# RMSNorm with each row written twice: engines issue in written order, and the last tile is loaded and stored in halves

## The chip, the cores and the metric

One core of one Trainium2 chip. The metric is the device time of one execution in microseconds (us). The kernel before takes 240.31 us, the median of 3 runs (239.82 to 240.62).

## The reference

```python
def reference(x, gamma):                     # x: 8 x 512 x 2048 f32
    x_rep = np.repeat(x, 2, axis=1)
    rms = np.sqrt((x_rep ** 2).mean(axis=-1, keepdims=True) + 1e-6)
    x_norm = x_rep / rms
    return (x_norm * gamma[None, None, :]).astype(np.float32)   # 8 x 1024 x 2048 f32
```

Every row is normalized and appears twice in the output. So 33.6 MB must be read and 67.1 MB written, whatever the kernel does in between.

## The kernel before

The 4096 rows are cut into 8 tiles of 128 partitions x 4 rows. A buffer `y` has 8 row slots for each partition: a tile is loaded into slots 4 to 7, and its 8 output rows are built in place in slots 0 to 7, so that one store moves 64 KB of consecutive bytes for each partition. There are three such buffers. (In the code `K = 4` is the rows of a partition in a tile and `R = 2` the copies of each row.) ACT (the scalar engine) squares and sums a row and takes the root, DVE (the vector engine) takes the reciprocal and scales; ACT copies three of the four rows, DVE the last.

```python
    load(0, parts=K)                       # K = 4, R = 2; load() issues on nc.sync
    # ... gamma to all partitions, eps ...
    load(1)
    load(2)
    for i in range(ntiles):                # 8 tiles
        y = ys[i]
        for k in range(K):
            xk = y[:, K * (R - 1) + k, :]
            y0, y1 = y[:, R * k, :], y[:, R * k + 1, :]
            # ... sq, ss, rms, rstd ...
            nc.scalar.activation(out=sq[:], in_=xk, func=Act.Square, accum_out=ss[:])
            nc.scalar.activation(out=rms[:], in_=ss[:], func=Act.Sqrt, scale=inv_d, bias=eps_t[:])
            nc.vector.reciprocal(out=rstd[:], in_=rms[:])
            nc.vector.scalar_tensor_tensor(out=y0, in0=xk, scalar=rstd[:], in1=gamma_b[:],
                                           op0=Alu.mult, op1=Alu.mult)
            if k == K - 1:
                nc.vector.tensor_copy(out=y1, in_=y0)
            else:
                nc.scalar.copy(out=y1, in_=y0)
        nc.sync.dma_start(out=out_t[i], in_=y.rearrange("p j d -> p (j d)"))
        if i >= 1 and i + 2 < ntiles:
            load(i + 2)
```

SyncE (SP) issues the large transfers, which run one after another in one queue, q1, on 16 DMA engines. A packet is the piece of a transfer that one DMA engine moves at a time; a transfer has landed when all its packets are done. Slack is how much earlier a transfer is issued than the engines run out of earlier work.

A scheduler decides in which order each engine issues these instructions. On ACT it had chosen, for most tiles: square, root, square, root, square, copy, copy, root, square, root, copy.

Of the kernel before, what the change touches and what calls it, by code (L numbers as in the profile page):

```python
# [1 line left out]

# [4 lines left out]


@with_exitstack
def kernel(  # L10
    ctx: ExitStack,
    tc: tile.TileContext,
    x: bass.AP,
    gamma: bass.AP,
    out: bass.AP,
):
    nc = tc.nc
    P = nc.NUM_PARTITIONS
    f32 = mybir.dt.float32
    Act = mybir.ActivationFunctionType  # L20
    Alu = mybir.AluOpType

    B, S, D = x.shape
    Bo, So, Do = out.shape
    R = So // S
    assert R == 2 and D == Do and B == Bo and So == S * R
    eps = 1e-6
    inv_d = 1.0 / float(D)


    K = 4
    N = B * S
    assert N % (P * K) == 0
    ntiles = N // (P * K)
    x_t = x.rearrange("b s d -> (b s) d").rearrange("(n p k) d -> n p k d", p=P, k=K)
    out_t = out.rearrange("b s d -> (b s) d").rearrange("(n p j) d -> n p (j d)", p=P, j=K * R)

    singles = ctx.enter_context(tc.tile_pool(name="singles", bufs=1))
    rows = ctx.enter_context(tc.tile_pool(name="rows", bufs=3))
    junk = ctx.enter_context(tc.tile_pool(name="junk", bufs=1, space=bass.MemoryType.PSUM))  # L40
    small = ctx.enter_context(tc.tile_pool(name="small", bufs=8))

    ys = []

    def load(i, parts=1):


        y = rows.tile([P, K * R, D], f32, name="y")
        step = K // parts
        for k in range(0, K, step):  # L50
            at = K * (R - 1) + k
            nc.sync.dma_start(out=y[:, at : at + step, :], in_=x_t[i, :, k : k + step, :])  # L52
        ys.append(y)

    load(0, parts=K)
    gamma_b = singles.tile([P, D], f32, name="gamma_b")
    nc.scalar.dma_start(out=gamma_b[0:1, :], in_=gamma.partition_broadcast(1))
    nc.gpsimd.partition_broadcast(out_ap=gamma_b[:], in_ap=gamma_b[0:1, :])  # L58
    eps_t = singles.tile([P, 1], f32, name="eps_t")
    nc.vector.memset(eps_t, eps)  # L60
    load(1)
    load(2)

    for i in range(ntiles):
        y = ys[i]
        for k in range(K):
            xk = y[:, K * (R - 1) + k, :]
            y0, y1 = y[:, R * k, :], y[:, R * k + 1, :]
            sq = junk.tile([P, D], f32, name="sq")
            ss = small.tile([P, 1], f32, name="ss")  # L70
            nc.scalar.activation(out=sq[:], in_=xk, func=Act.Square, accum_out=ss[:])  # L71
            rms = small.tile([P, 1], f32, name="rms")
            nc.scalar.activation(out=rms[:], in_=ss[:], func=Act.Sqrt, scale=inv_d, bias=eps_t[:])  # L73
            rstd = small.tile([P, 1], f32, name="rstd")
            nc.vector.reciprocal(out=rstd[:], in_=rms[:])  # L75
            nc.vector.scalar_tensor_tensor(  # L76
                out=y0, in0=xk, scalar=rstd[:], in1=gamma_b[:],
                op0=Alu.mult, op1=Alu.mult,
            )
            if k == K - 1:  # L80
                nc.vector.tensor_copy(out=y1, in_=y0)  # L81
            else:
                nc.scalar.copy(out=y1, in_=y0)  # L83
        nc.sync.dma_start(out=out_t[i], in_=y.rearrange("p j d -> p (j d)"))  # L84
        if i >= 1 and i + 2 < ntiles:
            load(i + 2)


# [1 line left out]
_INS = ['x', 'gamma']  # L90
_OUTS = [((8, 1024, 2048), 'float32')]


# [23 lines left out]
```

## Time and profile before

| What | Value | Where it is read |
|---|---|---|
| span of the profiled run | 239.1 us | page |
| busy: DMA queue q1, ACT, DVE | 98.3%, 49%, 37% | page |
| bytes moved, mean rate | 100.69 MB, 421 GB/s | page |
| one 64 KB packet on one DMA engine | 2.418 us (median of 1024) | packet records of the trace |
| last landing of load 7; last store issued | 199.38; 215.97 us | timeline |

From the page of the kernel before: the span; busy time, share and number of instructions of ACT; the DMA busy tenths in 40 slices; the DMA queues; and the chain that ended last.

```profile
span 239.1 us, 293 instructions
...
DVE 88.8 (37%) x73; ACT 116.3 (49%) x122; POOL 2.5 (1%) x5
...
DMA  7999998989899999899898999899989899898984
...
q1 hardware_dynamic: 2736, 100.66, 98.3%
...
HBM read 33.56 MB, written 67.11 MB: 421 GB/s over the span
## 4 chain that ended last, share of the span: by engine, by line
DMA 68%; ACT 13%; DVE 8%; SPq 1%; issue 1%
```

The chain gives ACT and DVE 21% of the span. It would be wrong to read this as 50 us to be won: the chain follows one path back, and while ACT and DVE work on it the DMA slices still show 8 or 9 tenths, since transfers issued earlier are draining. q1's 98.3% says how little time has no transfer.

The SyncE's timeline of the kernel before (start, duration, instruction) shows how far ahead transfers are issued:

```profile
98.53 0.33 SPq L84 DMA_DIRECT2D out_dram<-y  x1
101.38 0.34 SPq L52 DMA_DIRECT2D y<-in_x_dram  x1
127.68 0.33 SPq L84 DMA_DIRECT2D out_dram<-y  x1
...
215.97 0.33 SPq L84 DMA_DIRECT2D out_dram<-y  x1
```

Store 3 is issued at 98.53, while store 2 and load 4 lie ahead of it in the same queue and keep the engines until 110 us. The last line is different: store 7 is issued at 215.97 and the engines finish store 6 between 216.4 and 218.3 us. It is the only store with hardly any slack. The page's slices are too coarse to show it, and a table by windows books a whole packet at one moment. So the busy engines were counted from the starts and durations in the packet records; this is such a count, in half microseconds from 215.0 us:

```
before   215.0-: 16.0  16.0  15.8  11.0  15.8  16.0  16.0  16.0   engines of 16
```

### The profile page before, as it was taken

To read this page: it belongs to the slowest core of one execution; us is meant where nothing else is said; L and a number is where in the kernel's file an instruction comes from. 1 tells how busy PE (TensorE), PEld (TensorE's weight loads), DVE (VectorE), ACT (ScalarE), POOL (GpSimd) and SP (SyncE) were. 2 spreads that over 40 slices of the span, in tenths; PEclk is the share of its full clock that TensorE was granted. 3 is DMA by queue.
4 is the path that set the end of the run, shared out by engine and by line. 5 is a ranking of instruction groups with operands and counts; after the bars stand their busy time and mean duration, and the time that the engine had idled before them with its cause. 6 is when DMAs were issued, how large, how long until landed. Compare 5 with 4: busy or idle time off the path is not lost.

```text
span 239.1 us, 293 instructions
## 1 busy us (share of the span) xinstructions
DVE 88.8 (37%) x73; ACT 116.3 (49%) x122; POOL 2.5 (1%) x5
## 2 busy tenths in 40 slices
DVE  0449759590000085400863016820168202591000
ACT  2998999950000299104990059800598006970000
POOL 4000000000000000000000000000000000000000
DMA  7999998989899999899898999899989899898984
GB/s 262 426 454 439 439 439 351 526 351 526 351 428 439 493 395 451 384 411 510 362 515 351 439 439 506 373 422 433 493 384 471 362 461 461 384 482 384 493 384 175
DMA packets 2741, 100.69 MB, mean 421 GB/s; under 512 B 306, under 2 KB 306, under 8 KB 306
## 3 DMA queue, kind: packets, MB, share of 16 engines
q1 hardware_dynamic: 2736, 100.66, 98.3%
q14 instruction: 3, 0.02, 0.0%
q10 hardware_dynamic: 2, 0.01, 0.0%
HBM read 33.56 MB, written 67.11 MB: 421 GB/s over the span
## 4 chain that ended last, share of the span: by engine, by line
DMA 68%; ACT 13%; DVE 8%; SPq 1%; issue 1%
DMA y<-in_x_dram 41%; DMA out_dram<-y 27%; ACT sq L71 7%; DVE y L76 6%; ACT y L83 5%; DVE y L81 2%; SPq L52 1%; ACT rms L73 1%; DVE rstd L75 0%; SPq L84 0%
## 5 line engine op out<-in xcount | busy, mean ns | idle before, releaser
L71 ACT ACTIVATE sq<-y 128x2048 f32<-128x2048 f32 x32 | 59.7, 1865 | 92.5 <-DMA y<-in_x_dram 92.5
L76 DVE SCALAR_TENSOR_TENSOR y<-y,rstd,gamma_b 128x2048 f32<-128x2048 f32 x32 | 75.3, 2352 | 1.2
L75 DVE RECIPROCAL rstd<-rms 128x1 f32<-128x1 f32 x32 | 5.1, 159 | 124.8 <-ACT rms L73 124.8
L83 ACT COPY y<-y 128x2048 f32<-128x2048 f32 x24 | 44.7, 1890 | 3.2 <-DVE y L76 3.2
L81 DVE COPY y<-y 128x2048 f32<-128x2048 f32 x8 | 9.8, 1226 | 0.3
L73 ACT ACTIVATE rms<-ss,eps_t 128x1 f32<-128x1 f32 x32 | 9.4, 293 | 0.7
L71 ACT ACTIVATION_READ_ACCUMULATOR sq<-y 128x1 f32 x32 | 6.0, 186 | 0.0
L58 POOL PARTITION_BROADCAST gamma_b<-gamma_b x1 | 2.3, 2293 | 2.1 <-DMA gamma_b<-in_gamma_dram 2.1
L71 ACT ACT_TABLE_LOAD x1 | 1.3, 1283 | 1.3 <-PEq L101 1.3
L73 ACT ACT_TABLE_LOAD x1 | 1.3, 1283 | 0.0
L60 DVE MEMSET eps_t<- 128x1 f32 x1 | 0.1, 59 | 0.8 <-PEq L101 0.8
L101 POOL MEMSET const-bfloat16-1.0<- 128x1 bf16 x1 | 0.1, 101 | 0.0
L101 POOL MEMSET const-uint8-127<- 128x1 uint8 x1 | 0.1, 101 | 0.0
L101 POOL MEMSET const-float32-0.0<- 128x1 f32 x1 | 0.1, 98 | 0.2 <-issue 0.2
L101 POOL MEMSET const-float32-1.0<- 128x1 f32 x1 | 0.1, 99 | 0.0
## 6 DMA issues: line engine op xcount, KB each, us to landing
y<-in_x_dram SPq DMA_DIRECT2D x7, 4096.0 KB, 38.8
y<-in_x_dram SPq DMA_DIRECT2D x4, 1024.0 KB, 8.0
out_dram<-y SPq DMA_DIRECT2D x8, 32.0
gamma_b<-in_gamma_dram ACTq DMA_DIRECT2D x1, 8.0 KB
```

Source lines behind the costliest of these rows:

```text
L52: nc.sync.dma_start(out=y[:, at : at + step, :], in_=x_t[i, :, k : k + step, :])
L58: nc.gpsimd.partition_broadcast(out_ap=gamma_b[:], in_ap=gamma_b[0:1, :])
L60: nc.vector.memset(eps_t, eps)
L71: nc.scalar.activation(out=sq[:], in_=xk, func=Act.Square, accum_out=ss[:])
L73: nc.scalar.activation(out=rms[:], in_=ss[:], func=Act.Sqrt, scale=inv_d, bias=eps_t[:])
L75: nc.vector.reciprocal(out=rstd[:], in_=rms[:])
L76: nc.vector.scalar_tensor_tensor(out=y0, in0=xk, scalar=rstd[:], in1=gamma_b[:], op0=Alu.mult, op1=Alu.mult,)
L81: nc.vector.tensor_copy(out=y1, in_=y0)
L83: nc.scalar.copy(out=y1, in_=y0)
L101: nc = _bacc.Bacc("TRN2", target_bir_lowering=False, num_devices=1)
```

## The change

Its intent: with a fixed order on every engine, the square of row k+1 runs while DVE scales row k, so that ACT waits less; and with the last tile in halves, the final store can begin before the whole tile is done, and what remains at the end is half as long.

```diff
+    def compute(i, k0, k1):
+        rms = square(i, k0)                     # square and root on ACT
+        for k in range(k0, k1):
+            scale(i, k, rms)                    # reciprocal and scale on DVE
+            if k + 1 < k1:
+                rms = square(i, k + 1)
+                repeat(i, k, nc.scalar.copy)
+            else:
+                repeat(i, k, nc.vector.tensor_copy)
+
+    ctx.enter_context(tc.manual_schedule())
 ...
     for i in range(ntiles):
-        y = ys[i]
-        for k in range(K):
-            ... (the loop shown above)
-        nc.sync.dma_start(out=out_t[i], in_=y.rearrange("p j d -> p (j d)"))
+        parts = 2 if i == ntiles - 1 else 1
+        for k in range(0, K, K // parts):
+            compute(i, k, k + K // parts)
+            store(i, k, k + K // parts)
         if i >= 1 and i + 2 < ntiles:
-            load(i + 2)
+            load(i + 2, nc.sync, parts=2 if i + 3 == ntiles else 1)
```

(The small helpers `square`, `scale`, `repeat` and `store` hold the same instructions as before; `load` gets the issuing engine as an argument.) ACT's order becomes square, root, square, root, copy, square, root, copy, square, root, copy. SyncE's order of transfers stays as it was, apart from the halves.

More of the change, by code (lines that the diff above doesn't have):

```diff
@@ L43, with load @@
     ys = []
-    def load(i, parts=1):
+    def load(i, eng, parts=1):
         y = rows.tile([P, K * R, D], f32, name="y")
@@ L51, in load, with store, square, scale @@
             at = K * (R - 1) + k
-            nc.sync.dma_start(out=y[:, at : at + step, :], in_=x_t[i, :, k : k + step, :])
+            eng.dma_start(out=y[:, at : at + step, :], in_=x_t[i, :, k : k + step, :])
         ys.append(y)
-    load(0, parts=K)
+    def store(i, k0, k1):
+        nc.sync.dma_start(
+            out=out_t[i, :, R * k0 * D : R * k1 * D],
+            in_=ys[i][:, R * k0 : R * k1, :].rearrange("p j d -> p (j d)"),
+        )
+    def square(i, k):
+        sq = junk.tile([P, D], f32, name="sq")
+        ss = small.tile([P, 1], f32, name="ss")
+        nc.scalar.activation(
+            out=sq[:], in_=ys[i][:, K * (R - 1) + k, :], func=Act.Square, accum_out=ss[:]
+        )
+        rms = small.tile([P, 1], f32, name="rms")
+        nc.scalar.activation(out=rms[:], in_=ss[:], func=Act.Sqrt, scale=inv_d, bias=eps_t[:])
+        return rms
+    def scale(i, k, rms):
+        rstd = small.tile([P, 1], f32, name="rstd")
+        nc.vector.reciprocal(out=rstd[:], in_=rms[:])
+        nc.vector.scalar_tensor_tensor(
+            out=ys[i][:, R * k, :], in0=ys[i][:, K * (R - 1) + k, :], scalar=rstd[:], in1=gamma_b[:],
+            op0=Alu.mult, op1=Alu.mult,
+        )
+    def repeat(i, k, copy):
+        copy(out=ys[i][:, R * k + 1, :], in_=ys[i][:, R * k, :])
+    def compute(i, k0, k1):
[8 more added lines that the diff above has]
+    ctx.enter_context(tc.manual_schedule())
+    load(0, nc.sync, parts=K)
     gamma_b = singles.tile([P, D], f32, name="gamma_b")
@@ L60 @@
     nc.vector.memset(eps_t, eps)
-    load(1)
-    load(2)
+    load(1, nc.sync)
+    load(2, nc.sync)
     for i in range(ntiles):
-        y = ys[i]
-        for k in range(K):
-            xk = y[:, K * (R - 1) + k, :]
-            y0, y1 = y[:, R * k, :], y[:, R * k + 1, :]
-            sq = junk.tile([P, D], f32, name="sq")
-            ss = small.tile([P, 1], f32, name="ss")
-            nc.scalar.activation(out=sq[:], in_=xk, func=Act.Square, accum_out=ss[:])
-            rms = small.tile([P, 1], f32, name="rms")
-            nc.scalar.activation(out=rms[:], in_=ss[:], func=Act.Sqrt, scale=inv_d, bias=eps_t[:])
-            rstd = small.tile([P, 1], f32, name="rstd")
-            nc.vector.reciprocal(out=rstd[:], in_=rms[:])
-            nc.vector.scalar_tensor_tensor(
-                out=y0, in0=xk, scalar=rstd[:], in1=gamma_b[:],
-                op0=Alu.mult, op1=Alu.mult,
-            )
-            if k == K - 1:
-                nc.vector.tensor_copy(out=y1, in_=y0)
-            else:
-                nc.scalar.copy(out=y1, in_=y0)
-        nc.sync.dma_start(out=out_t[i], in_=y.rearrange("p j d -> p (j d)"))
+        parts = 2 if i == ntiles - 1 else 1
+        for k in range(0, K, K // parts):
+            compute(i, k, k + K // parts)
+            store(i, k, k + K // parts)
         if i >= 1 and i + 2 < ntiles:
-            load(i + 2)
+            load(i + 2, nc.sync, parts=2 if i + 3 == ntiles else 1)
 _INS = ['x', 'gamma']
```

## The prediction

> **What bounds the kernel now.** The DMA engines. The page gives 421 GB/s over a 239.1 us span; queue q1's packets take 98.3% of 16 engines' time; ACT is busy 49%, DVE 37%. The chain of waits is 68% DMA; its 13% ACT and 8% DVE run while earlier transfers still drain. In the packet records a 64 KB packet takes 2.418 us, a 32 KB packet 1.213 us: 27.1 GB/s for one engine, 434 GB/s for 16. The Trainium skill (DMA: Bandwidth & Descriptors, "Where 436 GB/s comes from") puts the ceiling at 435 GB/s; this trace agrees. 100.66 MB at 434 GB/s is 232 us. The rest of the span: first packet at 1.7 us; last packet ends at 237.7; last landing 238.0; about 1 us of ending; some slower packets.
>
> **Is the queue ever empty?** All bulk transfers share one queue, in order. A store costs nothing if issued before the transfers ahead of it have drained. From timeline and landings: store 0 is issued at 24.1 us, load 2 lands at 33; store 3 at 98.5, load 4 lands at 111; store 6 at 186.7, load 7 lands at 199.4. Slack is 9 to 13 us. Only the last store is tight: load 7 lands at 199.4, tile 7 takes 16.5 us, the store is issued at 216.0, and the engines finish store 6 between 216.4 and 218.3. Eleven of the engines then stand for 0.02 to 0.4 us: in the half microsecond from 216.5, 10.9 of 16 are busy, so the loss is about 0.2 us. The five latest engines have no gap there, and they end last (up to 237.7 us; the others near 236.2). So even this gap is not on the critical path.
>
> **What the change does.**
> 1. Written order: the transfers' order on SP stays, apart from the halves. From 2.0 us square, 0.29 root, 1.9 copy, 2.35 scale and 1.23 DVE copy I estimate about 17 us for a tile against 16.5 before, hidden behind 29 us of DMA per tile (9.8 load, 19.5 store). Worth 0.
> 2. Last tile in halves: the first half of load 7 lands about 5 us earlier; the half stores are issued near 203 and 209 us (estimates), so slack at the end grows from about 0.4 us to about 8. It removes the gap of the early engines; the late ones gain nothing. Worth 0 to 0.2 us.
> 3. Cost: the last tile's packets halve (load 32 to 16 KB, store 64 to 32 KB). Two 32 KB packets take 8 ns more than one of 64 KB, so 16 more packets per engine are some 0.13 us; two more completion packets 9 ns each.
> The bytes are unchanged: 33.56 MB read, 67.11 MB written.
>
> **Prediction.** 240.3 us, 80% range 239.5 to 241.1: within the spread of the runs (239.82 to 240.62). Faster by over 2%: 1%; within 2%: 98%; slower: 1%.
>
> **What would show the steps right or wrong.** GB/s near 421 and q1 near 98%; the dip of busy engines at 216.5 us is gone; last packet still between 236 and 238 us; ACT and DVE busy sums unchanged within 1 us; ends of the 16 engines still spread by 1 us or more.
>
> **What would make it wrong.** If a load came to wait for a store with the queue empty; if the 2.418 us packet depends on what ACT and DVE do meanwhile; if the spread of the engines' ends comes from the last transfers, so that halves shorten it by up to 1.5 us.

## The result, and the profile after

The changed kernel takes 240.34 us (median of 4 runs, 239.79 to 240.61), the kernel before in the same rounds 240.28 us. The ratio is 1.0001, 95% interval 0.9976 to 1.0026: the same. (A ratio here is the mean time of one kernel's fast runs over that of the other's fast runs of the same rounds, so not quite the ratio of the medians quoted.)

The same lines of the page, after:

```profile
span 238.8 us, 298 instructions
...
DVE 90.8 (38%) x74; ACT 115.6 (48%) x121; POOL 2.5 (1%) x5
...
DMA  7999998989899998999898999899998999898994
...
q1 hardware_dynamic: 3024, 100.66, 98.4%
...
HBM read 33.56 MB, written 67.11 MB: 422 GB/s over the span
## 4 chain that ended last, share of the span: by engine, by line
DMA 66%; ACT 13%; DVE 7%; SPq 1%; issue 0%
```

Nothing that bounds the kernel moved: same bytes, same rate. ACT has one copy less and DVE one more, since each half of the last tile ends with a copy on DVE. The SyncE's timeline after, the last stores:

```profile
202.50 0.34 SPq L56 DMA_DIRECT2D out_dram<-y  x1
...
209.25 0.33 SPq L56 DMA_DIRECT2D out_dram<-y  x1
```

The two halves of store 7 are issued at 202.50 and 209.25 us, where the kernel before issued it whole at 215.97. In both kernels the engines turn from store 6 to store 7 at 216.4 us or later, and all 16 have work now:

```
after    215.0-: 16.0  16.0  16.0  16.1  16.0  16.1  16.1  16.0   engines of 16 (a count over 16 is rounding at the seams)
```

So the change does what it intends: the final stores are ready 14 and 7 us earlier. They only stand longer in the queue. When each engine's last packet of a transfer ends (earliest, ninth and latest of 16):

```
                  load 7 done            store 6 done           last packet
before            197.12 197.38 199.03   216.44 216.74 218.35   236.21 236.29 237.66
after             197.08 197.49 198.86   216.40 216.81 218.18   235.76 236.18 237.54
```

In the changed kernel the latest engine is late already with load 7, and keeps its distance: the halves do not bring the ends of the 16 engines together (1.8 us apart after, 1.45 before), which the prediction had named as a way to be wrong.

### The profile page after: what moved, and what is told of

The parts are those of the page before. It is cut to its first block, busy times and chain, and to the rows that moved or that the text cites. A ratio compares the mean times of both kernels' runs of the same rounds, so it can differ in the third digit from the quotient of the medians.

```text
span 238.8 us, 298 instructions
## 1 busy us (share of the span) xinstructions
DVE 90.8 (38%) x74; ACT 115.6 (48%) x121; POOL 2.5 (1%) x5
## 4 chain that ended last, share of the span: by engine, by line
DMA 66%; ACT 13%; DVE 7%; SPq 1%; issue 0%
DMA y<-in_x_dram 39%; DMA out_dram<-y 27%; ACT sq L64 7%; DVE y L74 6%; ACT y L80 5%; ACT rms L68 1%; DVE y L80 1%; SPq L52 1%; DVE rstd L73 0%; SPq L56 0%
## 5 line engine op out<-in xcount | busy, mean ns | idle before, releaser
L80 ACT COPY y<-y 128x2048 f32<-128x2048 f32 x23 | 43.4, 1888 | 3.6 <-DVE y L74 3.6
L80 DVE COPY y<-y 128x2048 f32<-128x2048 f32 x9 | 11.0, 1227 | 0.3
```

Of the source, the lines that this page charges most:

```text
L80: copy(out=ys[i][:, R * k + 1, :], in_=ys[i][:, R * k, :])
```

## The experiments

Theory A: bytes through 16 DMA engines set the time, the queue of transfers is never empty to speak of, and both parts of the change act where nothing waits. Rival B: the parts have real effects that cancel. Rival C: the transfers are slowed by what ACT and DVE do, so the compute order could matter after all.

### The halves alone

```diff
-        nc.sync.dma_start(out=out_t[i], in_=y.rearrange("p j d -> p (j d)"))
+            parts = 2 if i == ntiles - 1 else 1         # in the row loop, scheduler kept
+            if (k + 1) % (K // parts) == 0:
+                nc.sync.dma_start(out=..., in_=...)     # the rows done so far
-            load(i + 2)
+            load(i + 2, parts=2 if i + 3 == ntiles else 1)
```

(As in the changed kernel, DVE copies the last row of each half of tile 7, so one copy moves from ACT to DVE.)

> The kernel before with only the last tile's load and store in halves (its own instruction order otherwise). Theory A (the DMA queue is never empty, so both parts of the change act where nothing waits): ratio to before 0.998 to 1.002, dip of busy engines at 216.5 us gone. Rival B (two real effects of opposite sign cancel): at least 0.5 us faster, ratio 0.998 or less.

Measured: 240.23 us against 240.39, ratio 0.9992 (0.9956 to 1.0029). The dip at 216.5 us is gone. The point estimate lies where A put it; the interval does not by itself exclude B's 0.5 us, which is 0.2%.

### Written order alone

```diff
-        parts = 2 if i == ntiles - 1 else 1
+        parts = 1
-            load(i + 2, nc.sync, parts=2 if i + 3 == ntiles else 1)
+            load(i + 2, nc.sync, parts=1)
```

> The changed kernel without the halves: written order alone. Its tile takes 17.0 us from landing to store against 16.6 before, so the last store is issued about 0.4 us later and the eleven early engines stand about 0.4 us longer near 216.5 us. Theory A: the late engines end the kernel, ratio 0.999 to 1.002. Rival B: at least 0.5 us slower, 1.002 or more, to balance the gain of the halves.

Measured: 240.43 us, ratio 0.9990 (0.9956 to 1.0024), in the same rounds as the halves alone. B needs this part to lose what the other wins; neither estimate goes the way B needs by more than a quarter of a microsecond. B's 0.5 us lies inside this interval too, so the times alone do not exclude it. What speaks against B are the packet records: the time in which an engine stands, from 4 us on to the last packet of the earliest engine, comes to 0.00 us of 16 engines with the halves alone and 0.03 with the written order alone (0.20 in the kernel before, 0.01 in the changed one), so there is no 0.5 us of it that one part could win and the other lose. One thing I expected did not happen: there was no dip of busy engines at all. In this run the last engine finished load 7 at 197.85 us instead of 199.03, so the last store was issued at 215.21 us, before anything ran dry:

```profile
215.21 0.33 SPq L56 DMA_DIRECT2D out_dram<-y  x1
```

The small gap of the kernel before is thus no fixed cost of an order. It depends on how late the latest engine is with load 7, and that differs from run to run: 199.03 us in the kernel before, and 199.57 in its version with added work in tile 7 (below), whose transfers are the same up to there.

### No square, root, scale or ACT copy (wrong result)

```diff
     def compute(i, k0, k1):
-        rms = square(i, k0)
-        ... (the row loop)
+        if k0 == 0:
+            for at in range(0, K, k1):
+                nc.vector.tensor_copy(out=ys[i][:, at : at + k1, :], in_=ys[i][:, K : K + k1, :])
```

> Wrong result on purpose: the changed kernel's transfers with no square, root, scale or ACT copy, only a DVE copy of the loaded rows per tile. Theory A (bytes through 16 engines bound it): 239.5 to 240.5 us, median 64 KB packet 2.418 us. Rival C (packets are slowed by ACT and DVE working on the same memory): over 1% faster, under 238 us, shorter packets.

Measured: 240.72 us, ratio 1.0005 (0.9969 to 1.0041). From its page:

```profile
span 237.5 us, 97 instructions
## 1 busy us (share of the span) xinstructions
DVE 35.5 (15%) x10; POOL 2.5 (1%) x5
...
q1 hardware_dynamic: 3024, 100.66, 98.7%
```

ACT does nothing and DVE 35 us of copies, and the kernel takes the same time; the median 64 KB packet is 2.418 us here too. (240.72 is 0.2 us above my range; so much do runs of one kernel differ in these rounds.) Rival C, at the 1% and more that it was put at, falls. A trace of it stays possible: packets above the usual duration of their size cost 1.67 us of 16 engines here, 2.12 in the changed kernel, and 0.45 us is 0.2%. This is also the bound on every change of compute order in this kernel that leaves the transfers as they are: with almost all compute gone, nothing is won that these runs can see.

### More ACT work in the last tile, four kernels

The four kernels differ in the two parts of the change and all square each row of tile 7 twice:

```diff
             nc.scalar.activation(out=sq[:], in_=xk, func=Act.Square, accum_out=ss[:])
+            if i == ntiles - 1:
+                nc.scalar.activation(out=sq[:], in_=xk, func=Act.Square, accum_out=ss[:])
```

The kernel before with it:

> The kernel before with each square of the last tile done twice, 4 x 1.87 = 7.5 us more of ACT there. Theory A: the slack of the last store is only about 0.4 us, and the late engines have up to 2 us more; so 5 to 7.5 us of it shows, 245 to 248 us. A rival (last tile's compute is hidden altogether): 240.3 us.

The changed kernel with it:

> The changed kernel with each square of the last tile done twice (7.5 us more of ACT). Theory A: the halves bought about 8 us of slack or more, so nothing shows: 240 to 241 us. If the halves bought no slack: 245 to 248 us, as the kernel before with the same load.

Written order without halves, with it:

> Written order without halves, squares of the last tile done twice. Theory A (slack comes from the halves alone): 245.5 to 248 us, like before with the same load or up to 0.5 us worse. If written order made the slack: near 240.3 us.

Halves without written order, with it:

> Halves without written order, squares of the last tile done twice. Theory A: 240 to 241 us, all hidden. If the halves need the written order to help: over 242 us.

Measured:

| | scheduler's order | written order |
|---|---|---|
| last tile whole | 248.92 us, ratio 1.0338 (1.0300 to 1.0375) | 247.33 us, 1.0301 (1.0261 to 1.0341) |
| last tile in halves | 241.68 us, 1.0041 (0.9987 to 1.0096) | 240.28 us, 1.0007 (0.9966 to 1.0048) |

(The first kernel ran on one chip, the other three together on another; each ratio is to the kernel before on its own chip.) With a whole last tile the added work shows; with halves it is hidden, in either order. So the halves did buy slack, and the order did not; without added work nobody asks for that slack. In the changed kernel with double squares the SyncE's timeline merges the two half stores of tile 7 into one line:

```profile
206.64 10.64 SPq L56 DMA_DIRECT2D out_dram<-y  x2
```

The second starts 0.33 us before the end of this stretch, at 216.95 us. The first engine has finished store 6 at 216.12, and still no engine stands, since the first half is there to be moved.

The 241.68 us of the halves in the scheduler's order lie above my range of 240 to 241. No gap explains them: in the profiled run (241.75 us) all 16 engines have work from store 6 to store 7. But one engine is late: the last packets end between 235.69 and 238.66 us. The profiled runs with all the bytes and no added gap differ mainly in this: in seven profiled kernels (before, changed, each part alone, without compute, and the two halves with double squares) the earliest engine ends at 235.5 to 236.2 us and the latest at 236.2 to 238.7, and the span is 1.3 to 1.4 us more than the latest. What makes one engine late stays open.

The kernel before lost 8.5 us with the added work, more than the 5 to 7.5 us that I expected. The DVE timeline of its last tile says why (the last column is the idle time before, and what ended it):

```profile
210.24 0.16 DVE L77 RECIPROCAL rstd<-rms 128x1 f32<-128x1 f32 x1 [3.36 <-ACT rms L75]
...
216.15 0.16 DVE L77 RECIPROCAL rstd<-rms 128x1 f32<-128x1 f32 x1 [3.36 <-ACT rms L75]
...
222.06 0.16 DVE L77 RECIPROCAL rstd<-rms 128x1 f32<-128x1 f32 x1 [3.36 <-ACT rms L75]
...
225.93 0.33 SPq L86 DMA_DIRECT2D out_dram<-y  x1
```

With the added instruction the scheduler chose another order, in which each row takes square, square, copy and root in a row, 5.91 us a row, and DVE waits 3.36 us of it. The tile takes 26.0 us (199.93 to 225.93) instead of 16.6. So the load was 9.4 us and not 7.5: a kernel whose order a scheduler chooses changes in more than the line that was edited. (In written order the tile took 24.6 us, 198.99 to 223.62, against 17.0: 7.6 more, as meant.) The windows of the same run show the queue empty for the 7 us before the store comes (columns: window, its length, DVE, ACT and POOL busy, clock, DMA share, GB/s):

```profile
216.00:219.00 3.00, 2.52 (x2) 2.97 (x4) 0.00 (x0) 1.00 0.05 22
219.00:226.00 7.00, 3.74 (x3) 3.03 (x4) 0.00 (x0) 1.00 0.00 0
226.00:229.00 3.00, 0.00 (x0) 0.00 (x0) 0.00 (x0) 1.00 0.82 350
```

The store was issued 9.96 us later than in the kernel before, its last packet 8.64 us later (246.30 against 237.66). The difference is the lateness of the slowest engine: after an empty queue all engines start together, and their last packets end within 0.14 us of each other, not 1.45.

### Fewer and more bytes

Half of two stores left out (wrong result):

```diff
-            store(i, k, k + K // parts)
+            store(i, k, k + K // parts if i not in (3, 4) else K // 2)
```

> Wrong result on purpose: the changed kernel with half of the stores of tiles 3 and 4 left out, 8.39 MB less, all compute kept. Theory A: 8.39 MB at 434 GB/s is 19.3 us, so about 221 us (220 to 222.5). If waits or compute bound it, less than 15 us would go: over 225 us.

Measured: 223.21 us, ratio 0.9283 (0.9239 to 0.9327); 16.8 us less by the medians, so 2 us above my range's middle and outside of it. The queue had no gap. The packet records hold a part of the miss: packets above the usual duration of their size cost 3.09 us of 16 engines, against 2.12 in the changed kernel. The excess over that kernel is in the last packets of store 5 (2.8 to 3.6 us for 2.418, at 165 us) and in load 7 behind it. In the profiled run the last packet ends at 218.72 us, 18.8 earlier than in the changed kernel, so the 1.0 us of slower packets leaves little of the 19.3 unexplained there. But it was the fastest of four (221.8 us), so what the others lost (222.9 to 223.6) is not seen.

One store done twice (result right):

```diff
             store(i, k, k + K // parts)
+            if i == 3:
+                store(i, k, k + K // parts)
```

> The changed kernel with tile 3 stored twice (same data, result still right): 8.39 MB more, 128 more 64 KB packets, 8 for each engine at 2.418 us. Theory A: 19.3 us more, about 259.6 us (259 to 260.5). If something other than the bytes set the time in the leaner kernel, where only 17 of 19.3 us went: clearly less or more than 19.3 us.

Measured: 263.24 us, ratio 1.0912 (1.0857 to 1.0968), 22 us more: outside my range. The experiment was flawed. From the waits of SyncE (who waited for whom: total us, times, longest) and the windows:

```profile
SPq L56 <- DMA out_dram<-y: 31.2, 1, 31.2
```
```profile
126.00:129.00 3.00, 2.13 (x2) 0.11 (x1) 0.00 (x0) 1.00 0.81 350
129.00:131.00 2.00, 0.00 (x0) 0.00 (x0) 0.00 (x0) 1.00 0.00 0
131.00:133.00 2.00, 0.00 (x0) 0.00 (x0) 0.00 (x0) 1.00 1.25 524
```

Both stores write the same rows, so the second had to wait until the first had landed, and the queue ran empty: 1.9 us of 16 engines by the packet records. Slowed packets cost 3.93 us, 1.8 more than in the changed kernel. The sum 19.3 + 1.9 + 1.8 = 23.0 us is close to the 22.7 us by which the last packet came later (260.24 against 237.54).

So a cleaner one: the added store sends tile 5's data to the rows of tile 3, long written (wrong result).

```diff
             store(i, k, k + K // parts)
+            if i == 5:
+                nc.sync.dma_start(out=out_t[3], in_=ys[5].rearrange("p j d -> p (j d)"))
```

> Wrong result on purpose: the run with tile 3 stored twice let its second store wait for the first to land (about 2 us with no transfer) because both wrote the same rows. Here the extra 8.39 MB store sends tile 5's data to the rows of tile 3, long written, so nothing waits. Theory A: 8 more packets of 2.418 us for each engine, ratio to before 1.080, plus up to 2 us for packets slowed where transfers meet (seen in both runs that changed the bytes): 259.3 to 262 us at a before of 240.3. If a store costs 22 us without a gap in the queue, Theory A's rate is wrong.

Measured: 259.56 us against 240.45, ratio 1.0803 (1.0773 to 1.0833), 19.1 us more. From its page:

```profile
span 257.7 us, 299 instructions
...
q1 hardware_dynamic: 3168, 109.05, 98.6%
```

Slowed packets cost 1.76 us, no more than elsewhere. An added store of 8.39 MB costs 8 packets of 2.418 us for each engine, and nothing else changes that the time shows: this is the bound, measured by itself. Why packets were slower in the two earlier runs stays open.

### The first store earlier

```diff
-        parts = 2 if i == ntiles - 1 else 1
+        parts = 2 if i == ntiles - 1 else K if i == 0 else 1
-            store(i, k, k + K // parts)
+            store(i, k, k + K // parts, nc.scalar if i == 0 else nc.sync)
```

> In all kernels so far, this with no square or scale too, the last packets of load 2, just ahead of the first store, take up to 2.3 us for 1.2, about 1 us of 16 engines. Here tile 0 is stored row by row from ACT's own queue from about 13 us on, so the first store runs while loads 1 and 2 do. If the loss belongs to the last packets of a load ahead of the first store, it is gone or moved: 239.2 to 240.3 us. If it is bound to that place in the input or that time, slow packets stay near 30 us and nothing changes: 240.3 us. In no case over 2% faster.

Measured: 241.31 us against 241.16 on its chip, ratio 1.0033 (0.9983 to 1.0084). The slow packets at 30 us are gone, so they belong to that place in the order of transfers and not to the time or the input. But slow packets appear elsewhere: 0.44 us at 15 to 17 us, 0.83 us at 77 to 82 us, 2.84 us in all. The loss moved, and the time did not fall.

No run that moves all the bytes was faster than the kernel before beyond its interval; the one that was faster left 8.39 MB out. I found no version that beats both kernels.

## Why the prediction was right

- **The bound.** Predicted: bytes at 434 GB/s through a queue that is never empty. Shown by removing the compute (ratio 1.0005) and by adding bytes (19.1 us for 8.39 MB, 19.3 predicted from the packet); taking the same bytes away won 16.8 us, of which the miss is explained only in part. As predicted, the trace agrees with the ceiling of 435 GB/s in the Trainium skill (DMA: Bandwidth & Descriptors, "Where 436 GB/s comes from"): 65536 bytes in 2.418 us on each of 16 engines is 434 GB/s. That the SBUF ports are what makes it, as the page says, no run here shows.
- **Written order, worth 0.** Right, 0.9990. The estimate of 17 us a tile was right too: tile 4 goes from the landing at 111.13 to the store at 128.13.
- **Halves, worth 0 to 0.2 us.** Right in effect. The predicted issue times, 203 and 209 us, were 202.50 and 209.25. The slack of "about 8 us" was mis-sized. I had held the second half against the end of store 6, but it is only needed when the first half ends, at 226.1 us: it has 17 us, and the first half has 14 (202.50 to 216.40). The double squares fit this: the second half came 0.8 us after the first engine had finished store 6, and nothing showed.
- **The gap.** I counted eleven engines that stood; a twelfth stood for 0.09 us. That the gap was off the critical path is seen in the end: it is gone, and the last packet ends at 237.54 instead of 237.66. What I took for a property of the kernel before depends on how late one engine is in that run, as the written order alone showed.
- **Cost of smaller packets, 0.13 us.** A 16 KB packet takes 0.611 us, so two take 0.009 us more than one of 32 KB; the summed packet time per engine rose from 234.95 to 235.02 us. Too small to be seen in the time.
- **One sign missed.** The sum of ACT and DVE busy time rose by 1.3 us (205.1 to 206.4), not under 1. I had overlooked that each half ends with a DVE copy, but that does not explain the rise: ACT's copies fell by 1.3 us (44.7 to 43.4) and DVE's rose by 1.2 (9.8 to 11.0). The pages count time in which two instructions of an engine overlap once. Summed one by one, the instructions of both engines took 213.2 us before and 212.8 after; so it is the overlap that shrank, not the work that grew.

Where did the intended gain go? Off the critical path. The chain after names ACT and DVE for 20% of the span (21% before), because a chain follows dependencies of one tile while the queue works on others.

## What to carry to other kernels

When one resource has work queued at all times, ask of every wait how long before its need the next piece is issued (here 9 to 13 us before the landing of the transfer ahead, for each store but the last): only a slack that is used up can be bought back. Test the bound directly, by removing the compute and by adding a known number of bytes, before reordering anything; and test a slack by adding work, which also shows what a change bought even if today's time does not show it. When an experiment adds a transfer or an instruction, look for the waits and the order that come with it, as two of these needed.

## What the Trainium skill lacked or had wrong

- DMA: Bandwidth & Descriptors, "Specifications", gives about 27 GiB/s for one engine. The unit does not fit: 65536 bytes in 2.418 us are 27.1 GB/s, which are 25.2 GiB/s; only the first agrees with 435 GB/s for 16.
- The same page, "Where 436 GB/s comes from", says without a condition that the HBM side (about 358 GB/s) binds transfers between HBM and SBUF. The condition stands in its section "Measured": a single core gets more, and about 358 only when the other core of its pair streams too. This kernel runs on one core; loading and storing, it averaged 421 to 424 GB/s over the whole span (before, changed, and without compute). Whether the neighbour was idle is not on record.
- The same page, "Latency and other measured facts", gives about 0.6 us to the first byte of a transfer issued by SyncE, and does not say from where it counts. With an empty queue, the first packet started 0.83 us after the issue began (225.93 to 226.77, and 223.62 to 224.45 in the run with written order and double squares), and 0.50 us after the issuing instruction, of 0.33 us, had ended.
- No page that I read has the packets that slow down where a load's last packets meet the next store. The last 32 KB packets of load 2 took 1.9 to 2.3 us for 1.213 in the kernel before, with or without compute, 0.8 to 1.0 us of 16 engines in each kernel with that order of transfers (with the packets just before them up to 1.3); with another order of transfers they were gone from there, and others were slow. The cause is not known.
- No page that I read says that the distance between the 16 engines can grow over many transfers while the queue is never empty: 0.6 us between first and last at load 0's first landing, 1.45 at the end of the kernel before (0.75 in the kernel with 97 instructions, 2.97 in that with halves, the scheduler's order and double squares). Two 8 KB packets on the instruction queue, at 90.5 and 148.8 us, are missing in that kernel; beside them single 64 KB packets took 2.55 and 2.80 us. That they cause the drift was not tested.
